# Sums of W_out's quadrants from small tiles loaded earlier, Q sums moved from GpSimd to VectorE, residual rows in the places of X's factors, one more raw tile and one more split pair

## The chip, the cores and the metric

The kernel runs on one core of a Trainium2 chip, in one launch. The metric is the device time in microseconds, the median over executions; the profile beside it is of one execution. The engines are named as in the profile: PE is TensorE, DVE VectorE, ACT ScalarE, POOL GpSimd, SP SyncE, which here only issues DMAs. Each engine, and each queue of DMA issues, takes its instructions in the order that they have in its program.

## The reference

One layer of a bidirectional encoder, on 1024 tokens of width 1024, in float32. Three sub-layers, each between two RMS norms and added to the residual: a SwiGLU FFN with half weight, a mixer (retention and neighbourhood attention), a second FFN with half weight. The change lies in the FFNs and around them:

```python
def _swiglu(x, w_in, w_out):
    g, u = jnp.split(x @ w_in, 2, axis=-1)
    return (jax.nn.silu(g) * u) @ w_out

h = _swiglu(_rms_norm(x, ffn1_pre_norm[l]), ffn1_w_in[l], ffn1_w_out[l])
x = x + 0.5 * _rms_norm(h, ffn1_post_norm[l])
m = _token_mixing(_rms_norm(x, mix_pre_norm[l]), w_mix_in[l], ...)
x = x + _rms_norm(m, mix_post_norm[l])
h = _swiglu(_rms_norm(x, ffn2_pre_norm[l]), ffn2_w_in[l], ffn2_w_out[l])
x = x + 0.5 * _rms_norm(h, ffn2_post_norm[l])
```

D_FF is 2816, so w_in has 1024 x 5632 elements and w_out 2816 x 1024.

## The kernel before

**Precision.** Every operand of a matmul is a pair: a high part (`h`), made by ScalarE's cast (L60), and a low part (`l`), made by VectorE as the difference (L61). A product of two pairs is three matmuls (`mm3`, L87 to L89). So each 128 x 512 piece of a weight costs ScalarE one cast and VectorE one subtraction before TensorE can use it. `raw` loads a weight into one of three tiles `wraw`; `piece` splits half of such a tile into one of eight pairs `wh`, `wl`.

**Seven products for eight.** Large products go by Strassen's scheme in Winograd's form: each matrix is cut into four quadrants, and with sums of quadrants (named s1 to s4 beside a11, a12, a22) seven products do, whose results are added up into the four quadrants of the output.

**First half of an FFN** (`ffn_in`, `Pairs.run`). X's factors are resident in SBUF (`Winograd`, tiles tagged `x`). There are 22 units, each of one gate piece and one up piece of W_in, 128 wide. A unit forms sums of its weight's quadrants on VectorE (L380, L381, L392, L401; the one at L381 in a tile `t2` of its own, which the profile calls `t`), runs seven products of 12 matmuls, and adds the results up on VectorE and ScalarE (L379 copies the first one out of its bank, so that the second can be added onto that bank). Of the first six units (four in the second FFN) two products are made ahead ("leads"), so they have five left; three leads are held in PSUM, the others saved, in the first FFN in six tiles `lead` of the pool `early`. `LeftFactors` then forms on GpSimd the sums of the unit's result (L447) and stores them to DRAM as left factors (`g0a`, `g0s` in the profile; `g1a`, `g1s` for the second FFN).

**Sums of W_out's quadrants** (`right_factors`). While `ffn_in` runs, the right factors of the second half are made: for each of 11 pieces, two 512 KB loads on SP's queue (L462, L463, tiles `wq`), four subtractions on VectorE (L468, L471, L474, L477) and four stores on GpSimd's queue (`w0s`, `w0a`, `w1s`, `w1a`). It is a generator: `Pairs.product` calls it once after each product's matmuls (`fin.side`), so a `yield` is one product of distance in the program; what is left at the end of `ffn_in` is drained there. `first` is the number of products before it begins.

**Second half** (`ffn_out`). Products a11, s1, s2, s3, a22, a12, s4 in this order, each of 11 steps (77 in all); a step loads and splits one piece of a left factor (`Blocks`: `graw`, `gh`, `gl`, L494) and one of a right factor (`raw` at L622 or L625), and does 12 matmuls for four blocks of 128 rows. `p1` to `p7` add the results up in tiles `q`. After the fourth product `more` (L576, L577) adds two pairs of Q on GpSimd, and `Epilogue.square` squares the sum on ScalarE (L519) and multiplies it by the gain on GpSimd (L520). `later` hands these pieces out one per step. `xload` loads the residual rows: rows 0 to 3 into two tiles that X's later factor a22 takes over, rows 4 to 6 into tiles `xr` of the epilogue's pool, row 7 into a `wraw` tile (L560); in the second FFN all eight go into four tiles. `Epilogue.steps` finishes a row (L530: scale and add; L541: the next norm), and `Winograd.put` turns the normed rows into X's factors for the mixer (L272 to L288).

**Order.** The program is written in order and a scheduler places it: on each engine, the earliest instruction in program order that its model holds ready goes next, so that an instruction from further on may be given to an engine earlier than it stands. A tile's place is taken again only when every use of the tile before is done, loads and stores too.

Of the kernel before, what the change touches and what calls it, by code (L numbers as in the profile page):

```python
# [10 lines left out]
F32 = mybir.dt.float32  # L11
F32R = mybir.dt.float32r
AF = mybir.ActivationFunctionType
ALU = mybir.AluOpType
# [4 lines left out]
P = 128  # L19
D = 1024  # L20
# [17 lines left out]
class Core:  # L38
# [28 lines left out]
        self.nc.gpsimd.dma_start(dst, src)  # L67

    def raw(self, src, n=D):
        raw = self.wpool.tile([P, D], F32, tag="wraw", name="wraw", bufs=3)  # L70
        self.nc.sync.dma_start(raw[:, :n], src)
        return raw

    def piece(self, src, eng=None):

        h = self.wpool.tile([P, 512], F32R, tag="wh", name="wh", bufs=8)
        l = self.wpool.tile([P, 512], F32R, tag="wl", name="wl", bufs=8)
        self.split(h, l, src, eng=eng)
        return h, l

# [218 lines left out]
class Pairs:  # L299
# [66 lines left out]
    def run(self, i, out, done, chain=False):  # L366

        c, nc = self.c, self.c.nc
        tt = nc.vector.tensor_tensor
        g, u = (c.raw(a) for a in self.srcs[i])  # L370
        b11, b21, b12, b22 = g[:, :512], g[:, 512:], u[:, :512], u[:, 512:]

        t1, t3, t4 = b11, b12, b21
        t2 = c.wpool.tile([P, 512], F32, tag="t2", name="t2", bufs=1)

        p1 = self.begun[i][0] if i in self.begun else self.product("a11", b11)
        c11 = out(0)
        for p, s in self.pieces(p1):
            nc.scalar.copy(c11[:, s], p)  # L379
# [12 lines left out]
        self.behind(tt(t3, b22, b12, ALU.subtract))  # L392
# [12 lines left out]
        p3 = self.product("s4", b22)  # L405
        tt(c12, p3, c12, ALU.add)
        done(2)
# [41 lines left out]
            c.store(self.dst[n][:, j * 512:(j + 1) * 512], a)  # L449


def right_factors(c, pool, w_out, dst, first):

    nc = c.nc
    tt = nc.vector.tensor_tensor

    for _ in range(first):
        yield
    for k in range(FT // 2):
        g, u = (pool.tile([P, D], F32, tag="wq", name="wq", bufs=2) for _ in range(2))  # L460
        t2 = pool.tile([P, 512], F32, tag="wt", name="wt", bufs=1)
        nc.sync.dma_start(g, w_out[k, 0])  # L462
        nc.sync.dma_start(u, w_out[k, 1])  # L463
        b11, b21, b12, b22 = g[:, :512], g[:, 512:], u[:, :512], u[:, 512:]
        yield
        yield
        yield
        tt(b11, b12, b11, ALU.subtract)  # L468
        c.store(dst["s1"][:, k * 512:(k + 1) * 512], b11)
        yield  # L470
        tt(t2, b22, b11, ALU.subtract)  # L471
        c.store(dst["s2"][:, k * 512:(k + 1) * 512], t2)
        yield
        tt(b12, b22, b12, ALU.subtract)  # L474
        c.store(dst["s3"][:, k * 512:(k + 1) * 512], b12)
        yield
        tt(b21, b21, t2, ALU.subtract)  # L477
        c.store(dst["a22"][:, k * 512:(k + 1) * 512], b21)
        yield
        yield  # L480


class Blocks:
# [16 lines left out]
class Epilogue:  # L500


    def __init__(self, c, pool, post, pre, resid, dst, put):
        self.c, self.pool, self.resid, self.dst, self.put = c, pool, resid, dst, put
# [40 lines left out]
def ffn_out(c, xtiles, spare, q, blocks, w_out, fac, gl, ep, side={}):  # L545


    nc = c.nc
    NK = FT // 2
    tt, add = nc.vector.tensor_tensor, nc.gpsimd.tensor_tensor  # L550
    later, rest, flips, xs = [], [], [], {}

    def xload(t):

        if t // 2 < len(xtiles):
            xs[t] = xtiles[t // 2][:, t % 2 * 2:t % 2 * 2 + 2].rearrange("p k f -> p (k f)")
        else:
            p, n = (ep.pool, "xr") if t < 7 else (c.wpool, "wraw")
            xs[t] = p.tile([P, D], F32, tag=n, name=n, bufs=3)
        nc.sync.dma_start(xs[t], ep.resid(t))  # L560

    def p1(u, b):
# [8 lines left out]
    def p7(u, b):  # L571
        tt(q[3][:, u], b, q[1][:, u], ALU.add)

        def more():
            xload(u)
            add(q[1][:, u], q[1][:, u], q[2][:, u], ALU.add)  # L576
            add(q[2][:, u], q[3][:, u], q[2][:, u], ALU.add)  # L577
            ep.square(u, 1, q[2][:, u], spare[u])
        later.extend((more, None))

# [16 lines left out]
    def p3(u, b):  # L597
        e = tt(q[1][:, u], b, q[1][:, u], ALU.add)
        out = q[1][:, u] if ep.pre is not None else q[3][:, u]
        ep.square(4 + u, 1, q[1][:, u], b if ep.pre is not None else spare[2 + u % 2], out, nc.vector if u == 3 else nc.gpsimd)  # L600
        g = ep.steps(4 + u, xs[4 + u], (q[0][:, u], out))
        next(g)
        rest.append(g)
        if u > 0:
            with c.tc.issue_after(e.ins):
                next(rest[u - 1])
        if u == 3:
            next(g)
        if ep.pre is not None:
            flips.extend(next(rest[j]) for j in ((), (), (0,), (1, 2, 3))[u])  # L610
        if u == 2 and 7 not in xs:
            xload(7)

    raws, quads = {}, {"a11": (0, 0), "a12": (1, 0), "s4": (1, 1)}

    def raw(n, k):
        if k % 2 == 0:
            m = min(2, NK - k)
            raws[n] = c.wpool.tile([P, D], F32, tag="wraw", name="wraw", bufs=3)
# [12 lines left out]

    def operand(n):
# [9 lines left out]
    for n, (i, k) in enumerate(steps):  # L643
# [8 lines left out]
        if later and i > 3:  # L652
            f = later.pop(0)
# [372 lines left out]
def trunk_layer(ctx: ExitStack, tc, x, g1a, w1i, w1o, g1b, gma, wmt, wnv, wrv, logits, dtab, rope, bias,  # L1026
                wro, wno, wmo, gmb, g2a, w2i, w2o, g2b, out):
    nc = tc.nc
# [5 lines left out]
    c = Core(tc, const, wpool, psum, dram)  # L1034
# [8 lines left out]
    wf = [{n: dt(f"w{i}{n}", [P, FT // 2 * 512]) for n in ("s1", "s2", "s3", "a22")} for i in range(2)]  # L1043
# [19 lines left out]
    early = pool(right, "early", "right")  # L1063
    wx = Winograd(c, (apool,) * 3, early, (14,) * 7)
    with tc.tile_pool(name="norm1", bufs=1) as ep:
        g = ep.tile([P, D], F32, tag="gpre", name="gpre", bufs=1)
        nc.sync.dma_start(g, g1a)
        for t in range(TT):
            xt = ep.tile([P, D], F32, tag="epx", name="epx", bufs=3)
            nc.sync.dma_start(xt, x[t * P:(t + 1) * P, :])  # L1070
            f = c.norm_T(xt, g, t, ep, wx.put)()
# [80 lines left out]
    for f, k in zip(rest, FLIP_FILL):  # L1152
        fill(k)
        f = f()
# [156 lines left out]
    with tc.tile_pool(name="ep2", bufs=1) as ep:  # L1311
# [4 lines left out]
        def save():  # L1316
            return [gs.tile([P, 384], F32, tag=n, name=n, bufs=3)[:, :256] for n in ("gh", "gl")]
# [98 lines left out]
```

## Time and profile before

| | |
|---|---|
| median of 3 runs | 2326.01 us (2325.84 to 2328.76) |
| profiled execution, own time | 2327.01 us |
| its span, first to last instruction | 2325.2 us |
| mean granted TensorE clock | 0.989 of full speed |
| PE busy | 2228.8 us (96%) |
| DVE busy | 1674.5 us (72%) |
| ACT busy | 1000.7 us (43%) |
| POOL busy | 626.8 us (27%) |

How to read it. The first products of the first FFN start at some 22 us; its first half ends at 470 us and its second at some 690; the mixer's projections follow until some 1045 us, attention, retention and the projections after them until some 1690, the second FFN's halves until 2103 and the end. A row of a list of waits names who waited, for whom, the total, how often and the longest. A row of an engine's course gives start, length, engine, line, operation, tiles written and read, and in brackets how long the engine had been idle and what ended it. A row by stretches gives for each engine the busy time and the number of instructions, and then the granted clock, the DMA engines' share and GB/s. A row of a line gives shortest, median and longest duration in ns, and first and last start.

### The profile page before, as it was taken

The page shows a single profiled execution, that of the slowest core. Times are in us where ns is not written, and L with a number is a line of the kernel's source. Part 1 is how long each engine was busy: PE and PEld are TensorE (multiplying, and loading weights), DVE is VectorE, ACT ScalarE, POOL GpSimd, SP SyncE. Part 2 cuts the span into 40 slices and gives each one's busy share as a digit, 9 for nine tenths or more (in the row PEclk, how much of TensorE's full clock was granted, in tenths as well). Part 3 has the DMA queues.
Part 4 walks back from the last instruction along what each step waited for, and adds up shares of the span by engine and source line. Part 5 has one row for each costly group of instructions (what it writes and reads, how often), then busy time and mean ns, then how long its engine had stood idle before and what let it go on. Part 6 is the DMA issues. An engine that isn't in the chain of part 4 may idle for free.

```text
span 2325.2 us, 30163 instructions
## 1 busy us (share of the span) xinstructions
PE 2228.8 (96%) x10288; PEld 1841.0 (79%) x10288; DVE 1674.5 (72%) x2887; ACT 1000.7 (43%) x2102; POOL 626.8 (27%) x713
## 2 busy tenths in 40 slices
PE   6999999999998999999999999999799999999998
PEld 5777888878786887778888888887577878887876
DVE  7997666655678768869876688547898766665566
ACT  6332233344464323248875675226533222234443
POOL 5443313110424134411101222101534432311042
PEclk9999999999999999999999999999899999999999
DMA  4666423386454542257745577856465633237665
GB/s 163 231 245 210 148 91 113 109 304 198 159 190 150 177 159 100 109 182 238 219 164 169 166 222 231 299 204 215 153 221 215 233 135 111 104 113 240 190 214 176
DMA packets 161179, 422.62 MB, mean 182 GB/s; under 512 B 19009, under 2 KB 46785, under 8 KB 160961
## 3 DMA queue, kind: packets, MB, share of 16 engines
q1 hardware_dynamic: 127584, 310.04, 41.1%
q0 software_dynamic: 33440, 110.65, 12.1%
q8 instruction: 81, 1.33, 0.2%
q14 instruction: 74, 0.60, 0.1%
HBM read 301.60 MB, written 123.21 MB: 183 GB/s over the span
## 4 chain that ended last, share of the span: by engine, by line
PE 62%; DVE 15%; issue 7%; DMA 5%; POOL 4%; ACT 3%; POOLq 0%; DVEq 0%; ACTq 0%; SPq 0%
PE ps L89 19%; PE ps L87 19%; PE ps L88 19%; DVE wl L61 3%; DMA wq<-in_dram 2%; PE pt L88 1%; PE pt L87 1%; PE pt L89 1%; DVE t L381 1%; ACT wh L60 1%; DMA w1a<-wq 1%; DVE gl L61 1%; DVE wraw L380 1%; POOL cmb L447 1%; POOL rstd L97 1%
## 5 line engine op out<-in xcount | busy, mean ns | idle before, releaser
L61 DVE TENSOR_TENSOR wl<-wraw,wh 128x512 fp32r<-128x512 f32 x662 | 488.5, 757 | 86.1 <-ACT wh L60 85.1
L60 ACT CAST wh<-wraw 128x512 fp32r<-128x512 f32 x670 | 390.7, 617 | 246.2 <-PE ps L88 80.0
L61 DVE TENSOR_TENSOR gl<-graw,gh 128x512 fp32r<-128x512 f32 (+2 forms) x178 | 133.3, 750 | 161.2 <-ACT gh L60 160.4
L87 PE MATMUL ps<-wh,gh 128*128 128x512 f32 x612 | 241.1, 396 | 7.3 <-ACT gh L60 6.2
L89 PE MATMUL ps<-wh,gl 128*128 128x512 f32 x612 | 240.6, 396 | 5.5 <-DVE gl L61 5.3
L88 PE MATMUL ps<-wl,gh 128*128 128x512 f32 x612 | 240.6, 394 | 2.0 <-DVE wl L61 2.0
L60 ACT CAST gh<-graw 128x512 fp32r<-128x512 f32 (+2 forms) x178 | 106.8, 601 | 197.2 <-PE ps L88 79.5
L87 PEld LDWEIGHTS ps<-wh,gh 128*128 128x128 f32 x612 | 116.3, 190 | 35.3 <-ACT gh L60 9.3
L89 PEld LDWEIGHTS ps<-wh,gl 128*128 128x128 f32 x612 | 115.8, 190 | 34.4 <-DVE gl L61 10.5
L88 PEld LDWEIGHTS ps<-wl,gh 128*128 128x128 f32 x612 | 116.4, 191 | 26.3 <-DVE wl L61 2.7
L60 ACT CAST wh<-t 128x512 fp32r<-128x512 f32 x58 | 36.0, 621 | 224.0 <-DVE t L381 220.7
L87 PE MATMUL ps<-a12h,wh 128*128 128x512 f32 x280 | 113.2, 404 | 10.3 <-ACT c L379 10.3
L395 DVE TENSOR_TENSOR c<-ps,gt 128x512 f32<-128x512 f32 x44 | 30.3, 688 | 124.7 <-PE ps L89 124.6
L89 PE MATMUL ps<-a12h,wl 128*128 128x512 f32 x280 | 111.8, 399 | 4.4 <-DVE wl L61 4.4
L87 PE MATMUL ps<-a11h,wh 128*128 128x512 f32 x280 | 111.7, 399 | 1.4 <-ACT wh L60 0.7
L88 PE MATMUL ps<-a12l,wh 128*128 128x512 f32 x280 | 111.2, 397 | 0.0
L89 PE MATMUL ps<-a11h,wl 128*128 128x512 f32 x280 | 110.2, 394 | 0.7 <-DVE wl L61 0.7
L88 PE MATMUL ps<-a11l,wh 128*128 128x512 f32 x280 | 110.4, 394 | 0.0
L87 PE MATMUL ps<-a22h,wh 128*128 128x512 f32 x280 | 109.8, 392 | 0.0
L89 PE MATMUL ps<-a22h,wl 128*128 128x512 f32 x280 | 109.1, 390 | 0.0
L88 PE MATMUL ps<-a22l,wh 128*128 128x512 f32 x280 | 109.1, 389 | 0.0
L97 POOL TENSOR_TENSOR rstd<-ss,mhalf 128x1 f32<-128x1 f32 x80 | 54.4, 683 | 162.6 <-DVE ss L951 55.4
(371 smaller groups left out, 5987.4 us busy)
## 6 DMA issues: line engine op xcount, KB each, us to landing
wraw<-in_dram SPq DMA_DIRECT2D x244, 512.0 KB, 4.4
wq<-in_dram SPq DMA_DIRECT2D x44, 512.0 KB, 4.0
g0s<-cmb POOLq DMA_DIRECT2D x44, 256.0 KB, 2.6
graw<-g0s SPq DMA_DIRECT2D x44, 256.0 KB, 2.9
g1s<-cmb POOLq DMA_DIRECT2D x44, 256.0 KB, 2.6
graw<-g1s SPq DMA_DIRECT2D x44, 256.0 KB, 2.7
bt<-in_dram SPq DMA_DIRECT2D x24, 384.0 KB, 3.6
g0a<-gt POOLq DMA_DIRECT2D x33, 256.0 KB, 2.5
```

The source lines that it names most:

```text
L60: nc.scalar.copy(h, src)
L61: (eng or nc.vector).tensor_tensor(l, src, hf, ALU.subtract)
L87: mm(ps, a[0], b[0], start=start, stop=False, skip_group_check=more)
L88: mm(ps, a[0], b[1], start=False, stop=False, skip_group_check=more)
L89: mm(ps, a[1], b[0], start=False, stop=stop, skip_group_check=more)
L97: self.nc.gpsimd.tensor_tensor(r[:, :n], ms, self.mhalf[:, :n], ALU.pow)
L380: self.behind(tt(t1, b12, b11, ALU.subtract))
L381: tt(t2, b22, t1, ALU.subtract)
L395: self.last = tt(c21, p7, c12, ALU.add).ins
L447: eng.tensor_tensor(s[o], a, b, op)
```

## The change

- `right_factors`: each quadrant of a piece is a 128 x 512 tile of its own, loaded by its own DMA of 256 KB (four for two), in the order in which the sums need them; five products of distance for three between loads and first sum; two or three products after the last. In the first FFN the five tiles come from the six `lead` tiles, and `first` is 35 for 21; in the second they come from five tiles `wq`, and `first` is 28.
- `more` in `ffn_out`: the two sums of Q on VectorE instead of GpSimd.
- Residual rows 4 to 7 of the first FFN: two more tiles with the tag of X's factors (`xt`), in places that s1's low part and s2's high part take later; loaded at steps 59, 62, 65 and 68 as in the second FFN. The `xr` tiles and row 7's use of a `wraw` tile go.
- `wraw` four tiles for three, `wh` and `wl` nine for eight, `t2` two for one.

```diff
     def raw(self, src, n=D):
-        raw = self.wpool.tile([P, D], F32, tag="wraw", name="wraw", bufs=3)
+        raw = self.wpool.tile([P, D], F32, tag="wraw", name="wraw", bufs=4)
...
-        h = self.wpool.tile([P, 512], F32R, tag="wh", name="wh", bufs=8)
-        l = self.wpool.tile([P, 512], F32R, tag="wl", name="wl", bufs=8)
+        h = self.wpool.tile([P, 512], F32R, tag="wh", name="wh", bufs=9)
+        l = self.wpool.tile([P, 512], F32R, tag="wl", name="wl", bufs=9)
...
-        t2 = c.wpool.tile([P, 512], F32, tag="t2", name="t2", bufs=1)
+        t2 = c.wpool.tile([P, 512], F32, tag="t2", name="t2", bufs=2)
...
-def right_factors(c, pool, w_out, dst, first):
+def right_factors(c, pool, tag, n, w_out, dst, first):
...
     for k in range(FT // 2):
-        g, u = (pool.tile([P, D], F32, tag="wq", name="wq", bufs=2) for _ in range(2))
-        t2 = pool.tile([P, 512], F32, tag="wt", name="wt", bufs=1)
-        nc.sync.dma_start(g, w_out[k, 0])
-        nc.sync.dma_start(u, w_out[k, 1])
-        b11, b21, b12, b22 = g[:, :512], g[:, 512:], u[:, :512], u[:, 512:]
-        yield
-        yield
-        yield
+        b11, b12, b22, b21, t2 = (pool.tile([P, 512], F32, tag=tag, name=tag, bufs=n) for _ in range(5))
+        for t, i, j in ((b11, 0, 0), (b12, 0, 1), (b22, 1, 1), (b21, 1, 0)):
+            nc.sync.dma_start(t, w_out[k, j, :, i * 512:(i + 1) * 512])
+        for _ in range(5):
+            yield
         tt(b11, b12, b11, ALU.subtract)
-        c.store(dst["s1"][:, k * 512:(k + 1) * 512], b11)
+        save("s1", k, b11)
         yield
...
-        yield
-        yield
+        for _ in range(3 if k % 2 else 2):
+            yield
...
-            xs[t] = xtiles[t // 2][:, t % 2 * 2:t % 2 * 2 + 2].rearrange("p k f -> p (k f)")
-        else:
-            p, n = (ep.pool, "xr") if t < 7 else (c.wpool, "wraw")
-            xs[t] = p.tile([P, D], F32, tag=n, name=n, bufs=3)
+        xs[t] = xtiles[t // 2][:, t % 2 * 2:t % 2 * 2 + 2].rearrange("p k f -> p (k f)")
...
             xload(u)
-            add(q[1][:, u], q[1][:, u], q[2][:, u], ALU.add)
-            add(q[2][:, u], q[3][:, u], q[2][:, u], ALU.add)
+            tt(q[1][:, u], q[1][:, u], q[2][:, u], ALU.add)
+            tt(q[2][:, u], q[3][:, u], q[2][:, u], ALU.add)
             ep.square(u, 1, q[2][:, u], spare[u])
...
-        if u == 2 and 7 not in xs:
-            xload(7)
...
-    xloads = {n: 4 + j for j, n in enumerate((68, 69, 70) if ep.pre is not None else (59, 62, 65, 68))}
+    xloads = {n: 4 + j for j, n in enumerate((59, 62, 65, 68))}
...
-        fin.side = Filler(right_factors(c, fp, w1o, wf[0], 21))
+        fin.side = Filler(right_factors(c, early, "lead", 6, w1o, wf[0], 35))
...
     xt = [x1pool.tile([P, 4, 512], F32, tag="x", name="x", bufs=2) for _ in range(2)]
+    xt += [spool.tile([P, 4, 512], F32, tag="x", name="x", bufs=8) for _ in range(2)]
...
-        fin.side = Filler(right_factors(c, fp, w2o, wf[1], 21))
+        fin.side = Filler(right_factors(c, fp, "wq", 5, w2o, wf[1], 28))
```

More of the change, by code (lines that the diff above doesn't have):

```diff
@@ L449, in __call__, with save @@
             c.store(self.dst[n][:, j * 512:(j + 1) * 512], a)
-def right_factors(c, pool, w_out, dst, first):
+def right_factors(c, pool, tag, n, w_out, dst, first):
     nc = c.nc
     tt = nc.vector.tensor_tensor
+    def save(n, k, t):
+        c.store(dst[n][:, k * 512:(k + 1) * 512], t)
     for _ in range(first):
@@ L459, in right_factors @@
     for k in range(FT // 2):
-        g, u = (pool.tile([P, D], F32, tag="wq", name="wq", bufs=2) for _ in range(2))
-        t2 = pool.tile([P, 512], F32, tag="wt", name="wt", bufs=1)
-        nc.sync.dma_start(g, w_out[k, 0])
-        nc.sync.dma_start(u, w_out[k, 1])
-        b11, b21, b12, b22 = g[:, :512], g[:, 512:], u[:, :512], u[:, 512:]
-        yield
-        yield
-        yield
+        b11, b12, b22, b21, t2 = (pool.tile([P, 512], F32, tag=tag, name=tag, bufs=n) for _ in range(5))
[3 more added lines that the diff above has]
+            yield
         tt(b11, b12, b11, ALU.subtract)
-        c.store(dst["s1"][:, k * 512:(k + 1) * 512], b11)
+        save("s1", k, b11)
         yield
         tt(t2, b22, b11, ALU.subtract)
-        c.store(dst["s2"][:, k * 512:(k + 1) * 512], t2)
+        save("s2", k, t2)
         yield
         tt(b12, b22, b12, ALU.subtract)
-        c.store(dst["s3"][:, k * 512:(k + 1) * 512], b12)
+        save("s3", k, b12)
         yield
         tt(b21, b21, t2, ALU.subtract)
-        c.store(dst["a22"][:, k * 512:(k + 1) * 512], b21)
-        yield
-        yield
+        save("a22", k, b21)
+        for _ in range(3 if k % 2 else 2):
+            yield
 class Blocks:
@@ L503, in __init__ @@
     def __init__(self, c, pool, post, pre, resid, dst, put):
-        self.c, self.pool, self.resid, self.dst, self.put = c, pool, resid, dst, put
+        self.c, self.resid, self.dst, self.put = c, resid, dst, put
         self.src = post, pre
@@ L549, in ffn_out @@
     NK = FT // 2
-    tt, add = nc.vector.tensor_tensor, nc.gpsimd.tensor_tensor
+    tt = nc.vector.tensor_tensor
     later, rest, flips, xs = [], [], [], {}
     def xload(t):
-        if t // 2 < len(xtiles):
-            xs[t] = xtiles[t // 2][:, t % 2 * 2:t % 2 * 2 + 2].rearrange("p k f -> p (k f)")
-        else:
-            p, n = (ep.pool, "xr") if t < 7 else (c.wpool, "wraw")
-            xs[t] = p.tile([P, D], F32, tag=n, name=n, bufs=3)
+        xs[t] = xtiles[t // 2][:, t % 2 * 2:t % 2 * 2 + 2].rearrange("p k f -> p (k f)")
         nc.sync.dma_start(xs[t], ep.resid(t))
@@ L618, in raw @@
             m = min(2, NK - k)
-            raws[n] = c.wpool.tile([P, D], F32, tag="wraw", name="wraw", bufs=3)
+            raws[n] = c.wpool.tile([P, D], F32, tag="wraw", name="wraw", bufs=4)
             if n in quads:
```

## The prediction

> **What bounds the kernel now.** I read the page's busy times first, then stretches of the run beside a full one, then the waits inside the stretches that are not full, engine by engine.
>
> ```profile
> span 2325.2 us, 30163 instructions
> PE 2228.8 (96%) x10288; PEld 1841.0 (79%) x10288; DVE 1674.5 (72%) x2887; ACT 1000.7 (43%) x2102; POOL 626.8 (27%) x713
> ```
>
> TensorE is the bound, and no matmul is added or removed. Only time in which it waits, or runs on half a clock behind a wait, can be won. How much that is per stage is read from the count of matmuls in a stretch (x after PE busy), because busy time hides the half clock:
>
> ```profile
> 105.00:205.00 100.00, 94.34 (x408) 76.22 (x407) 92.78 (x136) 30.43 (x54) 40.80 (x56) 0.99 0.65 228
> 205.00:255.00 50.00, 49.55 (x214) 40.54 (x213) 35.60 (x56) 13.44 (x25) 25.27 (x30) 0.98 0.58 208
> 255.00:305.00 50.00, 50.00 (x222) 41.39 (x222) 32.98 (x52) 15.35 (x28) 10.56 (x13) 1.00 0.35 124
> 1690.00:1740.00 50.00, 47.57 (x211) 39.05 (x210) 47.74 (x73) 17.15 (x30) 18.19 (x25) 1.00 0.65 237
> 1740.00:1790.00 50.00, 47.70 (x204) 39.02 (x203) 40.60 (x63) 15.12 (x27) 19.62 (x24) 0.97 0.64 235
> 1790.00:1840.00 50.00, 47.20 (x207) 38.38 (x206) 38.59 (x62) 14.60 (x26) 22.48 (x25) 1.00 0.55 197
> 1840.00:1890.00 50.00, 47.75 (x204) 39.01 (x203) 36.87 (x58) 13.98 (x25) 21.37 (x27) 0.97 0.56 205
> 601.00:612.00 11.00, 7.76 (x27) 5.18 (x26) 7.64 (x8) 6.29 (x14) 6.78 (x5) 0.91 0.24 67
> 2232.00:2242.00 10.00, 6.77 (x27) 4.46 (x26) 6.69 (x7) 5.89 (x14) 6.72 (x5) 1.00 0.31 94
> ```
>
> The third row is a full stretch: 222 matmuls in 50 us, 0.225 us each; the sums of W_out's quadrants are over by then. While they run in the first FFN (105 to 255 us) 622 are done where 666 fit: 44 x 0.225 = 9.9 us lost. In the second (1690 to 1890) 826 of 888: 62 x 0.225 = 14.0 us. The last two rows are the Q sums: 27 of 48.8 (4.9 us) and 27 of 44.4 (3.9 us).
>
> Why TensorE waits in the first group, at 189 to 204 us (SP's DMA queue, then DVE, then TensorE):
>
> ```profile
> 189.27 0.33 SPq L462 DMA_DIRECT2D wq<-in_dram  x1
> 189.97 1.04 SPq L463 DMA_DIRECT2D wq<-in_dram  x1
> 189.95 0.69 DVE L392 TENSOR_TENSOR wraw<-wraw 128x512 f32<-128x512 f32 x1
> 195.47 0.69 DVE L468 TENSOR_TENSOR wq<-wq 128x512 f32<-128x512 f32 x1 [4.83 <-DMA wq<-in_dram]
> 203.84 0.79 PE L87 MATMUL ps<-a12h,wh 128*128 128x512 f32 x1 [2.26 <-ACT c L379]
> 203.00:207.00 4.00, 3.16 (x8) 2.48 (x9) 3.97 (x7) 0.79 (x2) 3.93 (x2) 0.59 0.60 194
> SPq L462 <- DMA w1s<-wq: 89.5, 10, 15.7
> SPq L462 <- DMA w0s<-wq: 86.3, 10, 12.0
>   DMA wq<-in_dram: 25.4, 7
> ```
>
> DVE takes its instructions in order. The first sum of a piece (L468) stands ahead of the product's own sums and splits; it needs both 512 KB loads, and these wait on SP until the last piece's stores have left the same two tiles (rows w1s, w0s: 89.5 and 86.3 us of SP waiting). In all 7 such waits hold DVE 25.4 us. ScalarE's copy of the bank (L379) then comes late, and TensorE pays 2.26 us, and 4.00 x (1 - 0.59) = 1.6 us more in the four us after, at a granted clock of 0.59: one such stall is 3.9 us. It happens again in the second FFN.
>
> The second group:
>
> ```profile
> 604.77 1.73 POOL L577 TENSOR_TENSOR q<-q 128x512 f32<-128x512 f32 x1
> 606.53 0.63 ACT L519 ACTIVATE junk<-q 128x512 f32<-128x512 f32 x1 [4.12 <-POOL q L577]
> 607.79 1.37 DVE L61 TENSOR_TENSOR gl<-graw,gh 128x512 fp32r<-128x512 f32 x1 [2.44 <-ACT gh L60]
> 607.81 0.50 PE L87 MATMUL ps<-wh,gh 128*128 128x512 f32 x1 [1.54 <-ACT gh L60]
> L576 POOL TENSOR_TENSOR q<-q x8: 1288/1513/1747, 590.4 to 2231.5; 128x512 f32<-128x512 f32 x8
> L577 POOL TENSOR_TENSOR q<-q x8: 1283/1512/1743, 591.7 to 2235.7; 128x512 f32<-128x512 f32 x8
> 589.55 1.28 DVE L572 TENSOR_TENSOR q<-ps,q 128x512 f32<-128x512 f32 x2
> 593.50 3.47 DVE L61 TENSOR_TENSOR wl<-wraw,wh 128x512 fp32r<-128x512 f32 x2
> ```
>
> ScalarE's square of a Q sum stands in its queue ahead of the casts of the next operands and waits 4.12 us for POOL; the casts, DVE's low halves and TensorE follow. POOL has 8 sums of 1.5 us with 4 products by the gain between them. DVE beside POOL is slow as well: two splits take 3.47 us, two sums just before POOL starts 1.28 us.
>
> **The change, part by part.** The sum is against the profiled execution, whose own time is 2327.0 us (span 2325.2); the median of the runs is 2326.0, 0.04% less, so what is won is taken from the median.
>
> *Loads of W_out.* Yields only place the instructions in the program; an engine may be given them earlier, once tile and data are there:
>
> ```profile
> L462 SPq DMA_DIRECT2D wq<-in_dram x22: 327/328/328, 51.7 to 1862.0; - x22
> 70.95 0.40 PE L88 MATMUL ps<-s2l,wh 128*128 128x512 f32 x1
> wq<-in_dram SPq DMA_DIRECT2D x44, 512.0 KB, 4.0
> graw<-g0s SPq DMA_DIRECT2D x44, 256.0 KB, 2.9
> graw<-g1a SPq DMA_DIRECT2D x33, 256.0 KB, 3.8
> ```
>
> The first load goes at 51.7 us, before the first product (70.95), though 21 products stand ahead of it. So 21 to 35 or 28, and three yields to five, decide little; the tiles decide. Now a quadrant is a tile of its own: b22's is free as soon as s3 is formed, with no store in between, and b11's after s1's store, the first of the four, not after a22's, the last. The next piece's first sum needs two 256 KB loads, not 1 MB. By the nearest rows such a load lands in 2.9 to 3.8 us against 4.0: four issues for two cost SP 2 x 0.33 us a piece, beside idle SP time. In the first FFN the six tiles are those of the saved leads, which are used up by the products of units 3 to 5; so the sums leave the stretch of 105 to 145 us, where DVE is 92.78 busy of 100. Later there is room: 32.98 busy of 50 in the full row, and a piece adds 4 x 0.69 = 2.7 us, at one piece in 10 us 13.7 us, 46.7 of 50.
>
> Bounds, first FFN: 9.9 us won at best; at worst a new stall of the kind shown (3.9 us) at each of two places, -7.8. I take 6, nearest to the best, since the wait on the store goes but an in-order wait for the load stays possible. Second FFN: 14.0 at best, -7.8 at worst; its 5 tiles are a pool of their own, free from the start as now, so the 2.5 us of the first row remain, and each piece's last load still waits for a store. I take 6.
>
> The emission ends late in the first FFN: 35 + 105 steps ahead of the eleventh piece, of 142 products. Were it not pulled forward, its loads would go one product before the stage ends and DVE would wait there: one stall of 3.9. I take 1, because the 51.7 row shows the pull.
>
> *Q sums on DVE.* POOL loses 16 x 1.51 us, DVE gains 16 x 0.69 = 11.0 us, 5.5 per FFN spread over eight steps of 12 x 0.225 = 2.7 us, each with two splits of 0.69: 2.1 of 2.7 us, hidden. POOL keeps the products by the gain, but ScalarE's square no longer waits for POOL. The two stretches lose 4.9 + 3.9 = 8.8; bounds 0 (DVE's own queue delays the square) and 8.8; I take 8. Late next is the gain's product, needed only at the row's end.
>
> *Rows 4 to 7 of the residual.* They move into X's factor tiles, loaded from steps 59 to 68 instead of 68 to 70 and, for row 7, late into a raw tile:
>
> ```profile
> 676.96 0.33 SPq L560 DMA_DIRECT2D wraw<-in_dram  x1
> 709.05 3.29 SPq L71 DMA_DIRECT2D wraw<-in_dram  x2
> 712.72 0.45 PE L126 MATMUL pt<-ident,q 128*128 128x128 f32 x1 [3.34 <-DVE cmb L284]
> ```
>
> Row 7 holds a raw tile until 709.05, when the next weight's load goes. That wait goes. The new one: low s1 and high s2 take the tiles of rows 4 to 7, after their norms and stores; DVE's norms stand ahead of those splits already. TensorE's 3.34 us wait is for a bank that DVE must empty, so I count 1 of it; bounds -3.9 (s2's cast late, one stall) and 4.9 (3.34 and 1.6).
>
> *Fourth raw tile, ninth split pair, second t.* SP's longest wait and TensorE's two largest behind its transposes:
>
> ```profile
> SPq L71 <- DVE wl L61: 871.7, 164, 26.2
> PE ps L87 <- ACT c L379: 10.3, 7, 2.6
> PE ps L89 <- DVE wl L61: 8.9, 15, 1.6
> ```
>
> SP waits 871.7 us for a raw tile to come free, but TensorE's waits are for the bank's copy and for DVE's low halves, none for a raw load; the gain is taken as 0. It moves the whole order of loads, so the bounds are -3.9 and +3.9, one stall.
>
> Sum: 6 + 6 - 1 + 8 + 1 + 0 = 20 us. 2326 - 20 = 2306.
>
> *A rule weighed.* The low clock behind a 2.26 us wait is in the row above. The Trainium skill (TensorE: Matmul & The Clock Gate, What's actually happening) has the clock fall after an idle window of about 3.4 us; by that rule waits of 2.3 us would cost no clock. The trace disagrees, 0.59 after 2.26 us, and decides. Without the drops that four of the rows above hold (0.98, 0.91, and 0.97 twice) 4 x 1.6 = 6.4 us less would be there to win, 2312, which lies inside the forecast's own range.
>
> **The rivals.**
> *The stalls only move.* DVE's order may again put a first sum ahead of its load, as the 4.83 us row shows. Then both FFNs' 12 us are not won: 2326 - 8 = 2318. For it: the sums come as early as tiles allow. Against: one store less in the chain.
> *All of it goes.* DVE relieved and raw loads ahead win the upper bounds: 9.9 + 11.5 (14.0 less the 2.5 that remain) + 8.8 + 4.9 = 35, 2291.
> *Slower: SP's queue.* In the second FFN five tiles serve five; b21's load waits on SP for the last a22 store with the raw loads queued behind it. If a raw load thereby lands after its cast is due, each of 11 pieces costs one stall of 3.9: +43, less 14 for Q and the first FFN: 2355. It decides once SP's wait exceeds the lead that the fourth raw tile gives, half a unit, 0.5 x 7 x 12 x 0.225 = 9.5 us; today's longest is 15.7 us. Against: no wait of TensorE names a raw load though SP already waits 89.5 us there.
> *Small loads are dear.* If four loads ran one behind the other, 4 x 2.9 against 2 x 4.0 is 3.6 us more per piece; were a quarter of the 22 pieces' 79 us to reach TensorE, 20 us, only Q's 8 and row 7's 1 would stand against it: 2337. The Trainium skill (DMA: Bandwidth & Descriptors, Bandwidth) asks for transfers of 1 MiB or more. Against, as far as the trace goes: 256 KB lands sooner than 512 KB.
>
> **How the numbers follow.** Forecast 0.52, stalls move 0.20, all of it 0.13, a mixture that cancels within 0.2% (4.7 us, about what a measurement tells from no change) 0.05, SP's queue 0.07, small loads 0.03. The range reaches from the upper bounds, 2291, to a little beyond moved stalls, 2322. That leaves out the last two cases, half of the mixture and the outer part of the upper bounds. Faster by over 0.2%: all of 0.52 and 0.13 and most of 0.20, 0.81; same 0.09; slower 0.10. The forecast's own range is 2299 to 2313.
>
> **What would show it.** Right: over 215 matmuls in each 50 us of both FFNs' first halves; no DVE wait over 3 us on W_out's tiles; ScalarE's square waiting under 1 us; no drop of the clock near 608. Wrong: DVE waiting for a W_out load as long as now; raw casts waiting for loads; a new stall at the end of the first FFN's input half or where s2's cast takes row 7's tile; or new stalls in parts not touched (750 to 1690 us), from the new order.

## The result

The changed kernel is slower: 2359.78 us median (2356.57 to 2360.93) against 2326.31 of the kernel before on the same chip, ratio 1.014, 95% interval 1.0122 to 1.0157. That is 33 us lost where 20 were forecast to be won.

The profile's page of the changed kernel, its first lines:

```profile
span 2354.8 us, 30209 instructions
PE 2243.1 (95%) x10288; PEld 1852.2 (79%) x10288; DVE 1682.3 (71%) x2903; ACT 1001.3 (43%) x2102; POOL 600.0 (25%) x697
```

The same 10288 matmuls are 14.3 us longer busy (2243.1 for 2228.8), with no more work: the granted clock is lower (0.982 of full speed on the mean, for 0.989), and 2228.8 x 0.989 / 0.982 would be 15.9 us longer. The rest of the 29.6 us between the two profiled spans is waiting. Where, the count of matmuls in a stretch tells. The two first halves while W_out's sums run, before:

```profile
105.00:305.00 200.00, 193.89 (x841) 158.15 (x840) 161.37 (x242) 59.21 (x105) 76.63 (x97) 0.99 0.55 197
1690.00:1890.00 200.00, 190.21 (x820) 155.46 (x819) 163.80 (x254) 60.85 (x108) 81.65 (x100) 0.98 0.60 218
```

After; the last two rows are the stretches of the Q sums:

```profile
105.00:305.00 200.00, 180.42 (x743) 144.70 (x742) 154.08 (x230) 52.25 (x93) 78.46 (x101) 0.95 0.62 216
1690.00:1890.00 200.00, 179.45 (x752) 144.66 (x751) 163.75 (x246) 60.31 (x108) 79.54 (x97) 0.96 0.61 212
618.00:629.00 11.00, 11.00 (x51) 9.09 (x50) 11.00 (x12) 6.42 (x15) 6.10 (x4) 1.00 0.77 261
2254.00:2266.00 12.00, 12.00 (x54) 9.95 (x53) 12.00 (x17) 6.48 (x15) 3.95 (x3) 1.00 0.51 163
```

A full 200 us hold 884 matmuls (shown below by the tied kernel), 0.226 us each. The first halves now miss 141 and 132 where they missed 43 and 64. In the first FFN that is 98 x 0.226 = 22.2 us more. In the second FFN the changed kernel comes some 18 us later, so that stretches at the same times hold different work. The same 841 matmuls there, before and after:

```profile
1685.50:1890.50 205.00, 195.21 (x841) 159.57 (x840) 168.80 (x258) 62.53 (x110) 84.95 (x102) 0.98 0.58 213
```

```profile
1703.60:1921.10 217.50, 200.23 (x841) 162.36 (x840) 173.03 (x258) 62.25 (x110) 82.62 (x103) 0.96 0.58 201
```

They take 12.5 us more, so the two first halves lose some 35 us more than before. The Q sums lose nothing any more. The change to the second half of the first FFN is compared in the same way, from 20 us before the second half's first matmul (467.4 us before, 487.1 after) to 25 us behind it:

```profile
447.40:492.40 45.00, 43.29 (x183) 35.01 (x182) 28.39 (x40) 17.49 (x31) 9.19 (x11) 0.96 0.70 240
```

```profile
467.10:512.10 45.00, 41.51 (x170) 33.40 (x170) 26.95 (x39) 16.93 (x30) 9.18 (x11) 0.92 0.69 238
```

13 matmuls fewer are 2.9 us more lost there. VectorE's waits on W_out's tiles, from the list of waits of the changed kernel:

```profile
DVE lead L468 <- DMA lead<-in_dram: 19.8, 5, 8.0
DVE wq L468 <- DMA wq<-in_dram: 18.9, 4, 6.8
DVE lead L471 <- DMA lead<-in_dram: 14.4, 3, 6.6
DVE lead L471 <- DMA w0s<-lead: 2.8, 1, 2.8
DVE wq L471 <- DMA wq<-in_dram: 1.6, 2, 0.8
```

SP's waits with a small load (L465) for a store of sums, and the two of the kernel before that stand beside its rows of 89.5 and 86.3 us:

```profile
SPq L465 <- DMA w1s<-wq: 74.1, 30, 12.1
SPq L465 <- DMA w0s<-lead: 49.8, 17, 9.5
SPq L465 <- DMA w0a<-lead: 20.2, 6, 7.3
```

```profile
SPq L463 <- DMA w0a<-wq: 15.2, 10, 10.6
SPq L463 <- DMA w1a<-wq: 5.1, 10, 1.7
```

VectorE's five rows make 57.5 us in 15 waits (a sixth has 0.4 us), for 25.4 in 7 before. The longest is 8.0 for 4.8. Before, VectorE waited at the first sum of a piece alone (L468); now six of the 15 waits are at the second (L471), which has a load and a place of its own to wait for. SP's waits for stores don't tell the two kernels apart: 144.1 us for 196.1, with 53 of the 88 small loads for 40 of the 44 big ones. One of VectorE's places, in its course:

```profile
167.83 1.91 DVE L468 TENSOR_TENSOR lead<-lead 128x512 f32<-128x512 f32 x1 [4.07 <-DMA lead<-in_dram]
170.98 0.68 DVE L380 TENSOR_TENSOR wraw<-wraw 128x512 f32<-128x512 f32 x1
174.44 0.69 DVE L471 TENSOR_TENSOR lead<-lead 128x512 f32<-128x512 f32 x1 [2.78 <-DMA w0s<-lead]
175.05 0.68 DVE L381 TENSOR_TENSOR t<-wraw 128x512 f32<-128x512 f32 x1
```

SP's, ScalarE's and TensorE's courses at the same place, and then the stretch behind it:

```profile
161.20 15.05 SPq L465 DMA_DIRECT2D lead<-in_dram  x6
```

```profile
175.77 0.62 ACT L60 CAST wh<-t 128x512 fp32r<-128x512 f32 x1 [10.93 <-DVE t L381]
```

```profile
184.02 0.80 PE L87 MATMUL ps<-a12h,wh 128*128 128x512 f32 x1 [3.27 <-ACT c L379]
```

```profile
184.00:188.00 4.00, 3.98 (x9) 3.14 (x10) 3.96 (x8) 0.00 (x0) 1.08 (x2) 0.50 0.85 265
```

A first sum (L468) stands ahead of the weight's own sums (L380, L381) and waits 4.07 us for its load; then a second sum of the same piece (L471), between L380 and L381, waits 2.78 us for a place that a store has to leave. SP needs 15.05 us for six small loads. The weight's sum L381 is formed at 175.05, ScalarE has stood 10.93 us for it, its bank copy (L379) comes behind the casts, TensorE waits 3.27 us, and the clock in the four us after is 0.50. It is the chain that the prediction read at 203.84 in the trace before, with two waits on W_out in it instead of one.

The low clock follows a wait of 3.27 us here (0.50) and one of 2.26 us before (0.59). The Trainium skill (TensorE: Matmul & The Clock Gate, What's actually happening) gives a window of about 3.4 us; both waits are shorter, so the trace still disagrees.

### The profile page after: what moved, and what is told of

Its sections match the earlier page's. It is cut to its first block, busy times and chain, and to the rows that moved or that the text cites. A ratio compares the mean times of both kernels' runs of the same rounds, so it can differ in the third digit from the quotient of the medians.

```text
span 2354.8 us, 30209 instructions
## 1 busy us (share of the span) xinstructions
PE 2243.1 (95%) x10288; PEld 1852.2 (79%) x10288; DVE 1682.3 (71%) x2903; ACT 1001.3 (43%) x2102; POOL 600.0 (25%) x697
## 4 chain that ended last, share of the span: by engine, by line
PE 63%; DVE 15%; issue 8%; DMA 6%; POOL 5%; ACT 3%; DVEq 0%; POOLq 0%; SPq 0%; ACTq 0%
PE ps L89 19%; PE ps L88 19%; PE ps L87 19%; DVE wl L61 3%; POOL cmb L447 1%; PE pt L88 1%; PE pt L87 1%; PE pt L89 1%; DMA lead<-in_dram 1%; DMA wq<-in_dram 1%; DVE t L381 1%; DVE gt L422 1%; POOL rstd L97 1%; ACT wh L60 1%; DMA w1s<-wq 1%
## 5 line engine op out<-in xcount | busy, mean ns | idle before, releaser
L520 POOL TENSOR_TENSOR q<-q,gain 128x512 f32<-128x512 f32 x30 | 46.7, 1571 | 338.0 <-ACT junk L519 247.2
```

The costliest lines, as they stand in the source:

```text
L520: (eng or c.nc.gpsimd).tensor_tensor(h if out is None else out, h, self.post[:, b * 512:(b + 1) * 512], ALU.mult)
```

## The experiments

Theory A: the sums are given to VectorE as early as the scheduler's model has their loads landed, ahead of the products' own work, and with small tiles there are more places where that comes too early. Theory B: the larger pools reorder the loads. Theory C: 88 small loads for 44 large ones are dear as traffic. The kernels below are compared with the kernel before, run on the same chip.

**The new sums alone.** The kernel before with the new `right_factors` and its two calls, nothing else.

```diff
-def right_factors(c, pool, w_out, dst, first):
+def right_factors(c, pool, tag, n, w_out, dst, first):
...
-        fin.side = Filler(right_factors(c, fp, w1o, wf[0], 21))
+        fin.side = Filler(right_factors(c, early, "lead", 6, w1o, wf[0], 35))
```

> The kernel before with the new right_factors alone (small tiles, 35 and 28, five products of distance); Q sums, residual rows and pool sizes as before. Theory A, VectorE waits in order for W_out's small loads more often than for the two big ones: TensorE loses some 32 us in each FFN's first half, as in the changed kernel, against 10 and 16 before, so 2326 + 38 = about 2364 us, and the sums' waits on W_out tiles are 50 us or more in all. Theory B, the fourth raw tile, ninth pair and second t reorder the loads and are the loss: about 2326, within 6 us. Theory C, four 256 KB loads for two of 512 KB crowd the DMA engines: also slower, but with raw loads and left factors landing later, not only with waits of the sums.

2361.99 us against 2322.18, ratio 1.016 (1.014 to 1.0179).

```profile
105.00:305.00 200.00, 180.96 (x747) 145.28 (x746) 154.32 (x230) 52.65 (x94) 79.47 (x102) 0.95 0.61 218
1690.00:1890.00 200.00, 181.82 (x763) 147.28 (x762) 166.31 (x246) 60.73 (x108) 79.47 (x98) 0.96 0.61 216
```

The first halves lose about what they lose in the changed kernel (747 and 763 matmuls), and VectorE's waits on W_out's tiles are 54.1 us. Theory B falls as the cause of this loss; A and C stay.

**Q sums and residual rows alone.** The kernel before with `tt` for `add` in `more` and with the rows in `xt`; then the Q sums alone.

> The kernel before with the Q sums on VectorE and residual rows 4 to 7 in the places of X's factors; right_factors and pool sizes as before. Theory A and B alike: the stretches at 601 to 612 and 2232 to 2242 us lose nothing any more, 8.8 us won, 2317 us. If the rows cost what they save, the stall near 710 us grows by one stall of 3.9 and it ends near 2321.

> The kernel before with the sums of Q on VectorE alone; residual rows, W_out's loads and pools as before. The prediction's 8.8 us for Q and 1 for the rows: 8 to 10 us under the kernel before, 2316 to 2318, and the kernel with the rows as well within 2 us of it. Rival (the rows are worth the 4.9 us of the prediction's upper bound): 5 to 6 us under the kernel before.

Both: 2313.26 against 2322.18, ratio 0.9953 (0.9935 to 0.9971). Q alone: 2313.02 against 2323.9, ratio 0.9954 (0.9939 to 0.9968). So Q brings 10.9 us by the medians (7.4 to 14.2 by the interval), and the rows nothing that can be told.

**The changed kernel without the subtractions.** Raw quadrants are stored in the places of the sums, so this part of the computation is left out; loads and stores stay. A piece then takes four tiles for five, which lets loads go further ahead than in the changed kernel.

```diff
-        tt(b11, b12, b11, ALU.subtract)
...
-        tt(t2, b22, b11, ALU.subtract)
...
-        save("s2", k, t2)
+        save("s2", k, b22)
```

> The changed kernel without the four subtractions on W_out's quadrants: the quadrants are loaded and stored as they are, so the second halves multiply by wrong right factors; loads, stores and their bytes stay. Theory A: nothing on VectorE waits for these loads, so both first halves lose under 5 us each, 2360 - 50 = about 2310 us. Theory C: the DMA traffic is the same, so within 10 us of the changed kernel, 2350 or more. Theory B: the same, 2350 or more.

2342.71 us, ratio 1.0087 (1.0066 to 1.0108), far from theory A's 2310 and below the 2350 of B and C. The stretches:

```profile
105.00:305.00 200.00, 182.04 (x786) 149.46 (x785) 130.54 (x197) 56.17 (x99) 71.82 (x104) 0.96 0.62 221
1690.00:1890.00 200.00, 175.99 (x756) 144.19 (x755) 130.67 (x197) 58.18 (x102) 64.91 (x90) 0.94 0.58 201
```

One long wait, in SP's, ScalarE's and TensorE's courses:

```profile
169.23 9.76 SPq L465 DMA_DIRECT2D lead<-in_dram  x7
179.04 1.10 SPq L71 DMA_DIRECT2D wraw<-in_dram  x2
```

```profile
186.66 0.62 ACT L60 CAST wh<-wraw 128x512 fp32r<-128x512 f32 x1 [14.14 <-DMA wraw<-in_dram]
```

```profile
187.81 0.79 PE L87 MATMUL ps<-a12h,wh 128*128 128x512 f32 x1 [10.57 <-ACT c L379]
```

VectorE has no W_out work to wait in, but now the small loads follow each other so early that seven of them occupy SP's queue for 9.76 us, each waiting for a place, with the weight's raw loads behind: ScalarE's cast waits 14.14 us for a raw load and TensorE 10.57. This is the mechanism of the prediction's rival "SP's queue", in a kernel that isn't the changed one: there ScalarE's waits for raw loads are fewer than before. The row of the list of waits in the kernel before, in the changed one and in the one without subtractions:

```profile
ACT wh L60 <- DMA wraw<-in_dram: 35.6, 14, 6.7
```

```profile
ACT wh L60 <- DMA wraw<-in_dram: 13.4, 6, 7.0
```

```profile
ACT wh L60 <- DMA wraw<-in_dram: 55.0, 11, 14.3
```

The run takes away one wait and makes another, so it decides nothing between A and C; that early loads themselves can do harm on SP is read from it, not tested further.

**The sums tied.** The changed kernel, with each subtraction given an order (no semaphore) behind the newest of the products' own sums at its place in the program.

```diff
+    def tie(self, e):
+        if self.mark is not None:
+            self.c.tc.add_manual_dep(e.ins, self.mark.name, ... NoSync ...)
...
-        tt(c12, p6, c11, ALU.add)
+        self.mark = tt(c12, p6, c11, ALU.add).ins
...
-        tt(b11, b12, b11, ALU.subtract)
+        tie(tt(b11, b12, b11, ALU.subtract))
```

> The changed kernel with each of W_out's four subtractions held behind the newest sum of the products at its place in the program (an order on VectorE alone, no new wait on another engine), so that VectorE cannot be given it earlier than it stands; loads still go as soon as tiles are free. Theory A: loads land five products, 13 us, ahead, the sums wait for nothing, and the first halves lose under 6 us each; the last piece of the first FFN now comes at the end of the stage and costs one stall of about 4 to 8: 2360 - 50 + 6 = about 2316 us. Theories B and C: the order of these sums is not the cause, 2350 or more.

2299.43 against 2322.18, ratio 0.9893 (0.9873 to 0.9912): by the two ratios 57 us under the changed kernel, and better than theory A's 2316. The stretches; the third is, as above, from 20 us before the second half's first matmul (455.5 us) to 25 behind it:

```profile
105.00:305.00 200.00, 200.00 (x884) 165.46 (x883) 159.43 (x239) 61.79 (x109) 63.31 (x83) 1.00 0.48 171
1690.00:1890.00 200.00, 200.00 (x884) 165.62 (x883) 159.56 (x239) 61.35 (x110) 57.98 (x76) 1.00 0.44 154
435.50:480.50 45.00, 39.46 (x163) 31.80 (x163) 32.59 (x44) 15.87 (x29) 12.96 (x19) 0.92 0.85 290
```

SP's longest waits with a small load (L471 in this kernel):

```profile
SPq L471 <- DMA w1s<-wq: 147.0, 20, 17.1
SPq L471 <- DMA w0s<-lead: 115.4, 14, 14.5
```

The end of the first half, in VectorE's, GpSimd's and TensorE's courses:

```profile
458.10 3.38 DVE L480 TENSOR_TENSOR lead<-lead 128x512 f32<-128x512 f32 x1
```

```profile
458.43 2.49 POOL L453 TENSOR_TENSOR cmb<-gt 128x512 f32<-128x512 f32 x2
```

```profile
460.83 0.50 PE L87 MATMUL ps<-wh,gh 128*128 128x512 f32 x1 [2.46 <-ACT gh L60]
```

Both first halves are full, at full clock, and no wait of VectorE on W_out's loads is left in the list. The same 88 small loads and stores run, and SP waits more for stores than in the changed kernel (147.0 and 115.4 us): SP's waiting was not the cost, nor the small loads by their number. But the tie does two things: it keeps the sums behind the products' own work, and it spreads the pieces over the whole half (the last sum starts at 461.4 us, for 282.6 in the changed kernel), so that the stretch from 105 us carries 171 GB/s for 216. The next two runs part these. What is late next is the end of the first half: the last piece's sums are drained there, and 163 matmuls are done where the changed kernel does 170 and the kernel before 183.

**The tie without the small tiles.** The kernel before with the tie only: 512 KB loads, `wq` tiles and yields as they were.

> The kernel before with one edit: each subtraction of W_out's quadrants is held, by an order alone, behind the newest sum of the products; tiles, loads and yields as before. Theory A (the order on VectorE is the whole matter, the size of the tiles nothing): the 9.9 and 11.5 us that the two first halves lose before go, nothing else moves: 20 to 25 us under the kernel before, about 2303, with 220 matmuls or more in each 50 us of both first halves. Rival (the small tiles are what lets a held sum find its data; two 512 KB loads behind the stores of the last piece still come late): waits for wq of over 10 us in all remain, at most 10 us won.

2303.06 against 2325.49, ratio 0.9903 (0.9882 to 0.9923). The stretches, then VectorE's one row of waits for data of W_out:

```profile
105.00:305.00 200.00, 199.87 (x880) 164.85 (x880) 169.58 (x251) 62.11 (x110) 71.97 (x95) 1.00 0.56 198
1690.00:1890.00 200.00, 200.00 (x884) 165.64 (x884) 166.19 (x248) 62.45 (x112) 64.84 (x87) 1.00 0.52 183
```

```profile
DVE wq L474 <- DMA wq<-in_dram: 6.0, 4, 3.4
```

The whole of the first halves' loss goes with large tiles too, waits of 6.0 us in all are left, and the end of the half loses no more than before (190 matmuls in the 45 us around the change, for 183). In the first stretch there is as much traffic as before (198 GB/s for 197) and more work on VectorE (169.58 us for 161.37), so neither lighter traffic nor relief of VectorE won this: A is shown for the loss of the kernel before. The order is the matter; the size of the tiles brings nothing by itself.

**More small tiles, nothing tied.** The changed kernel with ten small tiles in each FFN, and with the pools of before.

```diff
-        fin.side = Filler(right_factors(c, early, "lead", 6, w1o, wf[0], 35))
+        fin.side = Filler(right_factors(c, early, "lead", 10, w1o, wf[0], 35))
...
-        fin.side = Filler(right_factors(c, fp, "wq", 5, w2o, wf[1], 28))
+        fin.side = Filler(right_factors(c, fp, "wq", 10, w2o, wf[1], 28))
```

> The changed kernel with the pools of before (three raw tiles, eight pairs, one t) and ten small tiles for six in the first FFN and for five in the second; nothing is tied. Theory A1 (a held-up sum is one whose load had itself to wait for its tile; with a second piece's tiles a load goes a piece ahead of its sums): VectorE's waits on W_out's loads fall from 63 us to under 20, the time to 2310 or less. Theory A2 (only the order counts: the scheduler gives sums and loads to the engines as soon as its model has them ready, however many tiles there are): the waits remain at 25 us or more, or weight loads are held up on SP behind small loads as in the kernel without sums, and the time is 2335 or more.

2319.15 against 2323.9, ratio 0.9971 (0.9959 to 0.9982): between the two expectations. The stretches, then VectorE's two longest rows of waits:

```profile
105.00:305.00 200.00, 194.19 (x838) 158.81 (x837) 163.93 (x245) 59.48 (x105) 79.14 (x100) 0.98 0.59 207
1690.00:1890.00 200.00, 190.44 (x816) 155.44 (x816) 163.44 (x248) 59.60 (x106) 72.55 (x96) 0.98 0.61 216
```

```profile
DVE lead L468 <- DMA lead<-in_dram: 10.7, 3, 4.4
DVE wq L468 <- DMA wq<-in_dram: 9.7, 3, 4.9
```

VectorE's waits on W_out's data fall to 22 us in all, and the first halves lose what they lost before the change (838 and 816 for 841 and 820), not less. So two things make up the loss. That there are waits at all comes from the order. That they last more than twice as long in the changed kernel comes from the number of tiles: the new sums alone, with the same pools of before, had 54.1 us of waits, 747 and 763 matmuls. It isn't the traffic: in the second FFN both kernels carry 216 GB/s, one with 816 matmuls and one with 763, so C falls. With six and five places for a piece of five 53 of the 88 small loads wait for a store, with ten places 22. That these late loads are the ones that VectorE then waits for is read from single places such as the one at 167.83, not shown for all.

**Yields of before.** The changed kernel with `first` 21 and three yields, two after the last sum.

> The changed kernel with the yields of before: first 21 in both FFNs, three products between loads and first sum, two after the last. The prediction's claim (yields only place instructions in the program, the tiles decide when they are given to an engine): within 4 us of the changed kernel, 2355 to 2364. Rival 1 (the place counts: three products of distance are less than five, so the sums wait longer): 2370 or more. Rival 2 (the small tiles alone are not the loss, the later beginning at 35 and 28 crowds the pieces): 2345 or less.

2353.84 against 2325.49, ratio 1.012 (1.0103 to 1.0137), 740 and 754 matmuls in the two stretches: that is 1 us outside the 2355 to 2364 of the prediction's claim and far from both rivals, so untied the distance in the program changes little, as the prediction had it.

**The tied kernel's end and its pools.** One kernel ends the pieces earlier (`first` 33, four yields and two), one has the pools of before.

> The tied kernel with the pieces a little earlier and closer, so that the eleventh ends before the first half does: first 33 for 35 in the first FFN, four products between loads and first sum for five, two after the last sum for two or three (9 products a piece, 33 + 99 = 132 of 142). Theory A: the two waits of 2.46 and 3.09 us at 458 and 462 go, the 8.3 us lost at the change to the second half become 2 or less, the 2.3 in the second FFN stay or go: 5 to 8 us under the tied kernel, ratio to before 0.986. Rival: the end of the half loses this time whatever the sums do, because the first factors of the second half have to be loaded and split there: within 2 us of the tied kernel.

> The tied kernel with the pools of before: three raw tiles, eight split pairs, one t. Theory: the wait of 4.89 us of TensorE for a low half at 875 in the mixer's projections (7.4 us lost there in every kernel with the larger pools, 1.4 in those without) comes from the larger pools and goes: 4 to 8 us under the tied kernel, first halves as full as there. Rival 1 (a fourth raw tile keeps the weight loads ahead in the first halves): 220 matmuls in 50 us no longer reached there, 2305 or more. Rival 2 (the pools do nothing, as the prediction has it): within 2 us of the tied kernel.

2298.7, ratio 0.9879 (0.9858 to 0.99), and 2298.19, ratio 0.9883 (0.9868 to 0.9899): neither can be told from the tied kernel's 0.9893. The earlier end does part of what was expected in its place, 183 matmuls for 163 in the 45 us around the change, 4.5 us, but a wait of 2.06 us stays there, and the 3 us between the two ratios are inside the intervals. With the larger pools TensorE waits in the mixer's projections; its course in the changed kernel (the tied one has the same wait of 4.89 us at 880.70):

```profile
909.36 0.79 PE L89 MATMUL ps<-a11h,wl 128*128 128x512 f32 x1 [4.88 <-DVE wl L61]
```

In the tied kernel with the pools of before this wait is gone; the longest two from 860 to 1000 us are 1.19 and 0.56 us. A gain in the sum of all stages isn't shown.

**Best of the parts.** The kernel before, the tie, Q on VectorE, and the rows; large tiles and pools as before.

> The kernel before with three edits: the subtractions of W_out's quadrants held by an order behind the newest sum of the products (tiles, loads and yields as before), the sums of Q on VectorE, and the residual rows in the places of X's factors; pools as before. If the parts add up, 22.4 us (the held sums alone) and 10.9 us (Q and rows alone): ratio 0.9855, some 2292, under every kernel so far. Rival: the tied kernel already holds both and the pools cost nothing, so the same 2299 to 2300 as there; the difference of 7 us would then have to be in the change to the second half (8.3 us lost there in the tied kernel, 2.3 in the kernel with held sums in big tiles).

2291.56 us against 2323.9, ratio 0.9854 (0.9838 to 0.9871): the parts add up, and it is faster than the kernel before and the changed one. The two stretches hold 881 and 884 matmuls. What the tied kernel lacks against it is found at the end of the first half, where the last sum starts at 363.1 us here, for 461.4 there; the 45 us around the change (second half's first matmul at 457.1 us):

```profile
437.10:482.10 45.00, 43.28 (x190) 35.17 (x190) 27.47 (x39) 17.64 (x32) 9.25 (x11) 1.00 0.67 232
```

190 matmuls for the tied kernel's 163 are 6.1 us, of the 9 us that the two ratios lie apart (0.9854 for 0.9893).

## Why the prediction was wrong

*W_out's loads, first and second FFN* (+6 and +6, worst -7.8 each): this step failed. Measured are -22.2 us (841 to 743 matmuls, x 0.226) and -12.5 (the same 841 matmuls, 217.5 us for 205.0). The mechanism had been read rightly in the trace before, an in-order wait of VectorE that ends in a bank copy and a low clock. What went wrong is the sentence "The wait on the store goes but an in-order wait for the load stays possible", and the bound that counted it at two places. The wait on the store did not go: 53 of the 88 small loads still wait for one (144.1 us), because five or six small tiles for a piece of five leave no room to load ahead; with ten it is 22 loads, and VectorE's waits are 22 us instead of 57.5. And a piece now has two sums at which VectorE stood waiting (nine waits at L468, six at L471) where it had one (seven at L468). The price of a stall was about right. The one at 184 us is dearer: 3.27 of waiting and, at a clock of 0.50 in the four us shown, at least 4.00 x (1 - 0.50) = 2.0 make 5.3, against 3.9. On the mean it stood: the 35 us that were lost in addition, with 8 waits more, are 4.3 us a wait. The number of places was wrong: 15 waits for 7, where the bound allowed two new ones in each FFN. The prediction saw that "the tiles decide" and that the sums come early, and did not draw from it that more and smaller tiles make more sums that come early. Its first sign of being wrong, VectorE waiting for a W_out load as long as now, came out twofold. The rival "The stalls only move" had the mechanism, but as a zero: it did not ask how often the stall would come. The rival "SP's queue" comes near the measured time with its 2355, but by a mechanism that the changed kernel doesn't show: ScalarE's waits for raw loads fell there, from 35.6 to 13.4 us.

*A load's landing* was taken as 2.9 to 3.8 us. The changed kernel's DMA issues have, at the median:

```profile
lead<-in_dram SPq DMA_DIRECT2D x44, 256.0 KB, 4.2
wq<-in_dram SPq DMA_DIRECT2D x44, 256.0 KB, 3.3
```

The first FFN's are beyond the upper bound and no sooner than the 4.0 us of twice the bytes. In the tied kernel the small loads cost TensorE nothing, so "Small loads are dear" isn't the reason. The Trainium skill's advice of 1 MiB and more (DMA: Bandwidth & Descriptors, Bandwidth) is not what decided here.

*The end of the half* (-1): the sums were pulled forward as argued and are over by 283 us, but before they were over by 255 already, and the change to the second half still loses 13 x 0.226 = 2.9 us more (TensorE's wait for ScalarE's `gh` is 2.38 us there, 1.18 before); why is not shown. The new sums alone, with the pools of before, have 183 matmuls there as the kernel before has. The other case, not pulled, is the tied kernel, which loses 20 x 0.226 = 4.5 us against the kernel before, about the one stall priced.

*Q sums* (+8): right, 10.9 by the medians with 8 inside the interval. ScalarE's square still waits for VectorE's sum (10.5 us in 6 waits, 3.0 at most, in the kernel with Q and rows alone), more than the "under 1 us" to be seen, but TensorE no longer waits: 51 matmuls in 11 us.

*Rows* (+1): within what can be told, 0. *Pools* (0, bounds 3.9): one new wait of 4.88 us, in a part not touched, which the last sentence of the prediction named as a way to be wrong; against the tied kernel with the old pools no difference of the whole is shown. *Yields* ("decide little"): right without the tie; with it they place the end of the sums.

Two readings of rows were off and changed nothing: VectorE's 92.78 of 100 us belongs to 105 to 205, not to 145, and the matmul at 70.95 is in the first product behind the leads, which began at some 22 us.

Sum of the measured terms: -22.2 - 12.5 - 2.9 + 10.9 + 0 - 4.9 = -31.6 us, against 29.6 lost between the spans. The two terms with the least direct evidence were taken near their best ends. That alone doesn't explain the sign and size: with both at their worst, -7.8 each, the sum is -7.8 - 7.8 - 1 + 8 + 1 = -7.6, or 2334 us. The bound itself, two new stalls of 3.9 us in each FFN, was too small.

## What to carry to other kernels

When side work that waits for loads shares an in-order engine with the work that feeds TensorE, ask where the scheduler will put it, not where the program has it: an order-only dependency on the main work's newest instruction was worth 22 us with nothing else changed. Splitting a load into smaller tiles, with no more room in all, multiplies the places where such work meets its data; count these places before pricing one stall. A list of waits of the transfer queue says little here: SP waits 262.4 us for stores of sums in the tied kernel, whose first halves are full, and 144.1 us in the changed one.

## What was not expected of the hardware

A 128x512 subtraction on VectorE took 3.38 us at 458.10 in the tied kernel, nearly five times the median of 0.68 us of its line; GpSimd ran two of its sums beside it, from 458.43 us on for 2.49 us. The longest single subtraction of W_out's quadrants in the trace before is 1.92 us. That GpSimd is the cause isn't shown: it is one record, and no run takes those sums away from that place.
